# The merge of the next block's inverses emitted ahead of a block's chain, in one layer of a hybrid attention and RWKV-7 encoder

## The chip, the core and the metric

The kernel runs on one core of one Trainium2 chip. Its time is the device time of one execution in microseconds (us); several executions give a median. A core has a matmul engine (TensorE, PE in the profile; its weight loads are shown apart as PEld), a vector engine (DVE), a scalar engine (ACT), GpSimd (POOL), and SyncE (SP), which issues DMA transfers. Each engine works through a queue of its own in order and waits on semaphores for the others.

## The reference

One layer of an encoder over 1024 positions of width 1024: a half-step SwiGLU feed-forward, then a mixing step in which one input projection feeds eight heads of dilated attention and eight heads of RWKV-7, then a second half-step feed-forward. The change lies in the RWKV-7 scan, which runs forward and backward over the sequence:

```python
def _rwkv7_step(state, inp):
    r, w, k, v, kk, kka = inp
    sa = jnp.einsum('dbhvk,dbhk->dbhv', state, kk)
    state = state * w[..., None, :] - sa[..., :, None] * kka[..., None, :] + v[..., :, None] * k[..., None, :]
    y = jnp.einsum('dbhvk,dbhk->dbhv', state, r)
    return state, y
...
    xs = (orient(both(r)), orient(decay), orient(k_dir), orient(both(v)),
          orient(both(kk)), orient(kk[:, :, None, :] * a))
    _, ys = lax.scan(_rwkv7_step, state0, xs)
...
    x = x + post2(concat(attn, rwkv) @ w_out)
```

The two directions' outputs are summed, normalised for each head, given a bonus term and multiplied by a gate (the finishing units below). Both groups then go through `w_out`.

## The kernel before

**The scan in chunks.** The step by step scan is worked in chunks of 64 positions, two chunks to a block, so eight blocks (`NB`), numbered in the order of the scan; both directions of a block are worked together. Inside a chunk the rule is a triangular system for each of the 16 pairs of head and direction. A block passes through four steps.

- *prep* (to L852): DVE and ACT scale the keys by the decays; PE multiplies them (`lp`, L836) and transposes them (`bp`, L844); DVE masks the products into `lm` (L838). The triangles go out to memory and come back as `X`.
- *solve* (L872 to L876): DVE inverts the 32 x 32 diagonal halves of all triangles in 31 steps of two operations, one after the other (`ttmp`, `Ti`); a last transpose (L876) leaves the inverses in `X` again. One solve is a long serial piece of DVE work.
- *merge* (L889 to L902): joins two 32 x 32 inverses to a 64 x 64 one for each of 32 triangles. On PE, 64 transposes (L889) write `pa`; ACT copies it to `tt` (L890); 32 products with the off-diagonal part `lm` go back to `pa` (L894); ACT copies those to `tt` (L896, two copies) and to `am` (L897); 32 products (L900) need both; ACT writes them negated into `tt` (L902, two copies). So PE and ACT alternate. There is one bank for `pa`, one `am`, and two `tt`, used in turn.
- *chain* (L923 to L972): the scan proper. At its start ACT copies part of `pr` into `lm` (L928, four copies; this part must wait until L894 has read its own). Then, for each of the two chunks: `xu` = state times `lm` (L941); ACT copies it to `xs` (L944); the state is started with `st` from `sv` (a helper at L937); `xu` again from `xs` and the merged inverse `tt` (L952); ACT writes `uv` (L954); more `y` and `st` from `uv` (L937); DVE scales `st` to the next state `sv` (L968); ACT copies `y` to `yb` (L970). A chain needs the chain before it through `sv`, and its own merge through `tt`.

The merge is written as follows, shortened:

```python
        tt = self.tt[n % 2]
        T.matmul(pa[r, j, :], D[r, j, :], self.ident[r, r], ...)            # L889, 64 of them
        A.copy(tt[:, :, 32:64], pa)                                         # L890
        T.matmul(pa[hi, j, :], lm[lo, par, d, i, pr, 32:64], D[lo, j, :])   # L894, 32
        A.copy(tt[lo, :, 0:32], pa[lo])                                     # L896, two halves
        A.copy(am, pa)                                                      # L897
        T.matmul(pa[lo, j, :], am[hi, j, :], tt[hi, j, 32:64])              # L900, 32
        A.activation(tt[lo, :, 32:64], pa[lo], AF.Copy, scale=-1.0)         # L902, two halves
```

**What else runs there.** `upto(n + 3)` emits prep and solve up to block n + 3 behind chain n. `project_attended` multiplies finished attention tiles by the upper half of `w_out` (`po`, L1064, large matmuls; inputs `yq`, `yah`, `yal` at L1075 to L1078; the result is copied to `yao` at L1083); its weights are loaded as `wor` and split into two parts `woh` and `wol` (L1054). Such tiles give PE work that needs no chain. Behind the loop come the finishing units: `yc` (L995), `var` (L1004), `bonus` (L1011), `rstd` (L1014), `gate` (L1025) on PE, with DVE and ACT steps between them (L996 to L1026, then a split at L186 and L187), and the lower half of `w_out`, whose weights come as `wor` and are split at L186 and L187 into `woh` and `wol`, for the products `pw` (L1064).

**What sets the order.** The program is written once, and a scheduler with a cost model places each instruction on its engine's queue: among what its model holds ready, the instruction that was emitted first goes first. So the place of a call in the loop is a rank and not a fixed position.

Of the kernel before, what the change touches and what calls it, by code (L numbers as in the profile page):

```python
# [163 lines left out]
class _Kernel:  # L164
# [1002 lines left out]
    def run(self):  # L1167
# [5 lines left out]
        with self.top as top:  # L1173
# [86 lines left out]
            NB, s_sr, s_pr, s_zr, s_pm = NC_ // BLK, ExitStack(), ExitStack(), ExitStack(), ExitStack()  # L1260
# [5 lines left out]
            pm = self.pool(s_pm, "ps_m", 1, space=PSUM, **R)  # L1266
# [4 lines left out]
            blk = {}  # L1271
# [7 lines left out]
            sc = self.pool(s_sc, "scan")  # L1279
# [9 lines left out]
            def upto(m):  # L1289
                while nxt[0] <= min(m, NB - 1):  # L1290
                    n = nxt[0]
                    blk[n] = self.prep(n, sp, pp, (R0, R1, B0)[n % 3])
                    blk[n]["inv"] = self.solve(n, sp)
                    nxt[0] += 1
# [3 lines left out]
            upto(2)  # L1298
            WA = self.out_weights(eo, 0, self.aog)
            for n in range(NB):  # L1300
                if n:
                    self.merge(n, blk[n], sc, pm)
                self.chain(n, blk.pop(n), sc, pc)
                upto(n + 3)
                for t in {0: [0, 1], 1: [2], 2: [3], 3: [4], 4: [5, 6], 5: [7]}.get(n, []):
                    self.project_attended(eo, sc, pe, t, WA, rs_a)
# [133 lines left out]
```

## Time and profile before

| | us |
|---|---|
| runs, median of 3 | 2345.42 (2341.84 to 2350.20) |
| the profiled execution | 2343.05 |
| its span, first to last instruction | 2341.3 |
| granted clock, mean | 0.969 |

The scan stage with its eight chains takes from about 1256 to 1563 us of the span, an eighth of the whole. The two feed-forward parts hold most of the rest, and the change emits nothing there. A row of the timeline gives the start, the length, the engine, the line, the operation, what is written and read, the shape, the number of records, and in brackets how long the engine stood idle before and what released it. A window row gives the busy time of each engine in a stretch, then the clock that PE was granted as a share of full speed, the busy share of the DMA engines, and what they moved.

### The profile page before, as it was taken

How to read it: one execution, taken by the hardware profiler on the slowest of the kernel's cores; microseconds unless marked ns; L12 is line 12 of the kernel's file. 1: busy time of each engine (PE TensorE's matmuls, PEld its weight loads, DVE VectorE, ACT ScalarE, POOL GpSimd, SP SyncE). 2: the span in 40 equal slices, each digit the busy share in tenths (PEclk: the TensorE clock that was granted, in tenths of full speed). 3: DMA queues.
4: the chain of work that ended last, by engine and by line, in shares of the span. 5: the costliest groups of instructions: out<-in, count | busy, mean ns of one | idle time of the engine just before them, and what ended most of it. 6: DMA issues, size and time to landing. Idle time of an engine off the chain costs nothing. (4 is left out here: it accounts for less than half of the span.)

```text
span 2341.3 us, 41376 instructions
## 1 busy us (share of the span) xinstructions
PE 2206.1 (94%) x15556; PEld 1783.6 (76%) x15556; DVE 1768.5 (76%) x2870; ACT 1031.8 (44%) x1958; POOL 551.5 (24%) x662
## 2 busy tenths in 40 slices
PE   6999999999999998999996998988799999999997
PEld 4788888878877676788775777765578888887886
DVE  8899999965676244666668877737899999996565
ACT  4323232354577412666555555454442323235443
POOL 6244444410000010111111111122424444441000
PEclk8999999999999999999997999989899999999999
DMA  5244545486672514443268655467435454548665
GB/s 154 97 165 167 171 148 172 153 269 191 195 229 83 219 46 123 119 115 99 62 174 222 174 155 161 113 205 267 154 113 170 168 171 147 173 154 269 193 191 178
DMA packets 357148, 381.97 MB, mean 163 GB/s; under 512 B 73042, under 2 KB 264402, under 8 KB 356948
## 3 DMA queue, kind: packets, MB, share of 16 engines
q1 hardware_dynamic: 309088, 278.53, 39.5%
q0 software_dynamic: 27504, 88.14, 9.9%
q10 hardware_dynamic: 20356, 12.66, 1.8%
q8 instruction: 122, 2.00, 0.4%
q14 instruction: 78, 0.64, 0.1%
HBM read 256.49 MB, written 122.75 MB: 162 GB/s over the span
## 5 line engine op out<-in xcount | busy, mean ns | idle before, releaser
L186 ACT ACTIVATE wh<-raw 128x512 fp32r<-128x512 f32 (+1 forms) x273 | 168.2, 627 | 271.2 <-DVE raw L62 93.6
L187 DVE TENSOR_TENSOR wl<-raw,wh 128x512 fp32r<-128x512 f32 (+1 forms) x273 | 278.7, 1023 | 6.0 <-ACT wh L186 5.2
L81 PE MATMUL gu<-xh,wh 128*128 128x512 f32 x704 | 278.3, 396 | 1.2 <-ACT xh L186 0.8
L81 PE MATMUL gu<-xl,wh 128*128 128x512 f32 x704 | 276.6, 393 | 0.0
L81 PE MATMUL gu<-xh,wl 128*128 128x512 f32 x704 | 276.2, 392 | 0.0
L415 PE MATMUL pd<-gl,gwh 128*128 128x512 f32 x616 | 240.3, 390 | 2.3 <-DVE gl L187 2.3
L415 PE MATMUL pd<-gh,gwh 128*128 128x512 f32 x616 | 239.5, 390 | 0.6 <-DVE row L86 0.6
L415 PE MATMUL pd<-gh,gwl 128*128 128x512 f32 x616 | 239.7, 389 | 0.0
L86 DVE TENSOR_TENSOR row<-gu,row 128x512 f32<-128x512 f32 x308 | 206.3, 681 | 23.9 <-PE gu L81 23.1
L187 DVE TENSOR_TENSOR gwl<-graw,gwh 128x512 fp32r<-128x512 f32 (+1 forms) x176 | 117.9, 672 | 127.7 <-ACT gwh L186 126.9
L116 POOL DMA_DIRECT2D d_hid<-row x154 | 84.7, 551 | 473.1 <-DVE row L114 447.6
L186 ACT ACTIVATE gwh<-graw 128x512 fp32r<-128x512 f32 (+1 forms) x176 | 101.4, 576 | 186.3 <-PE pd L415 154.3
L81 PEld LDWEIGHTS gu<-xh,wh 128*128 128x128 f32 x704 | 133.9, 190 | 30.1 <-ACT xh L186 2.0
L81 PEld LDWEIGHTS gu<-xl,wh 128*128 128x128 f32 x704 | 133.9, 190 | 27.7
L81 PEld LDWEIGHTS gu<-xh,wl 128*128 128x128 f32 x704 | 133.5, 190 | 27.9
L415 PEld LDWEIGHTS pd<-gl,gwh 128*128 128x128 f32 x616 | 115.6, 188 | 27.4 <-DVE gl L187 3.7
L415 PEld LDWEIGHTS pd<-gh,gwh 128*128 128x128 f32 x616 | 115.5, 188 | 25.3 <-DVE row L86 1.0
L415 PEld LDWEIGHTS pd<-gh,gwl 128*128 128x128 f32 x616 | 115.7, 188 | 24.0
L187 DVE TENSOR_TENSOR gl<-raw,gh 128x512 fp32r<-128x512 f32 x160 | 113.6, 722 | 18.1 <-ACT gh L186 17.7
L94 ACT ACTIVATE row<-row 128x512 f32<-128x512 f32 x44 | 27.9, 633 | 221.6 <-DVE row L86 214.1
L145 POOL TENSOR_TENSOR ws<-ws 128x512 f32<-128x512 f32 x88 | 114.3, 1299 | 1.2
L186 ACT ACTIVATE gh<-raw 128x512 fp32r<-128x512 f32 x160 | 98.0, 621 | 35.3 <-DMA raw<-in_ffn_w_down_dram 25.5
(354 smaller groups left out, 5254.3 us busy)
## 6 DMA issues: line engine op xcount, KB each, us to landing
d_hid<-row POOLq DMA_DIRECT2D x154, 256.0 KB, 2.4
graw<-d_hid SPq DMA_DIRECT2D x132, 256.0 KB, 3.2
raw<-in_ffn_w_gate_dram SPq DMA_DIRECT2D x88, 256.0 KB, 3.1
raw<-in_ffn_w_up_dram SPq DMA_DIRECT2D x88, 256.0 KB, 3.4
ws<-in_ffn_w_down_dram SPq DMA_DIRECT2D x88, 256.0 KB, 4.6
d_ws<-ws POOLq DMA_DIRECT2D x88, 256.0 KB, 2.3
raw<-d_ws SPq DMA_DIRECT2D x88, 256.0 KB, 2.9
raw<-in_ffn_w_down_dram SPq DMA_DIRECT2D x66, 256.0 KB, 3.5
```

The source lines that it names most:

```text
L81: self.K.nc.tensor.matmul(ps, a[:, k, :], b[:, k, :], start=(k == 0 and i == 0), stop=(k == 3 and i == 2))
L86: add = lambda o, x: V.tensor_tensor(o, ps, x, op=OP.add)
L94: A.activation(y[:, 0], y[:, 0], AF.Silu)
L116: put = lambda n, y: G.dma_start(self.hid[n - 1, j // 2], y)
L145: G.tensor_tensor(o, a, b, op=OP.subtract)
L186: self.nc.scalar.activation(h, src, AF.Copy)
L187: (eng or self.nc.vector).tensor_tensor(l, src, h, op=OP.subtract)
L415: T.matmul(ps[x], a[:, ts], b, start=(m == 0 and k == 0), stop=(m == NM - 1 and k == 2))
```

## The change

In the loop over blocks, block n's own merge is no longer emitted ahead of its chain. Block n + 1's is emitted there, so that of the two it is the merge that ranks first. Merge 0 stands ahead of the loop in both. No instruction is added or left out.

```diff
             for n in range(NB):
-                if n:
-                    self.merge(n, blk[n], sc, pm)
+                if n + 1 < NB:
+                    self.merge(n + 1, blk[n + 1], sc, pm)
                 self.chain(n, blk.pop(n), sc, pc)
                 upto(n + 3)
```

Three places in the queues. First PE's queue at the end of the scan. Before, these rows lead from the end of chain 6 (`sv_15958` is the state that it leaves) to chain 7 (`xu_16206`), with merge 7 (`pa_16059`) between them:

```order
L937 MATMUL y_15963<-lm_14420,uv_15955 64x64 x16
L889 MATMUL pa_16059<-ident_62,X_15164 32x32 x4
L937 MATMUL st_16207<-sv_15958,ident_62 64x256 x4
L937 MATMUL y_16208<-pr_15033,sv_15958 64x64 x8
L937 MATMUL y_16208<-pr_15101,sv_15958 64x64 x8
L894 MATMUL pa_16059<-X_15164,lm_15022 32x32 x32
L941 MATMUL xu_16206<-sv_15958,lm_15022 64x64
L900 MATMUL pa_16059<-tt1_11964,am_16058 32x32 x32
L941 MATMUL xu_16206<-sv_15958,lm_15022 64x64 x15
L995 MATMUL yc_16432<-f_y0_16418,k_cen_6989 128x512
L952 MATMUL xu_16206<-xs_16225,tt1_11964 64x64 x16
```

In the changed kernel merge 7 (now `pa_15849`) lies in the first chunk of chain 6 (`y_15998`, `st_15997`), and the second piece shows the end of chain 6 with chain 7 (`xu_16206`) right behind it:

```order
L889 MATMUL pa_15849<-ident_62,X_15300 32x32 x64
L952 MATMUL xu_15996<-xs_16015,tt0_11963 64x64 x2
L937 MATMUL y_15998<-pr_14635,sv_15704 64x64 x5
L894 MATMUL pa_15849<-X_15300,lm_15158 32x32 x32
L937 MATMUL st_15997<-uv_15990,bt_14581 64x64
L937 MATMUL y_15998<-lm_14556,uv_15990 64x64
L937 MATMUL st_15997<-uv_15990,bt_14581 64x64 x7
L937 MATMUL st_15997<-uv_15990,bt_14649 64x64 x8
L937 MATMUL y_15998<-lm_14556,uv_15990 64x64 x8
L900 MATMUL pa_15849<-tt1_11964,am_15848 32x32 x32
```

```order
L937 MATMUL st_16098<-uv_16091,bt_14649 64x64 x8
L937 MATMUL y_16099<-lm_14556,uv_16091 64x64 x15
L941 MATMUL xu_16206<-sv_16094,lm_15158 64x64 x16
L937 MATMUL st_16207<-sv_16094,ident_62 64x256 x4
L937 MATMUL y_16208<-pr_15169,sv_16094 64x64 x5
L952 MATMUL xu_16206<-xs_16225,tt1_11964 64x64 x16
```

The merge's last two steps moved ahead by a whole chain, the same holds for merges 1 to 6, and `yc` of the first finishing unit is no longer in chain 7's first chunk: one `yc` stands in its second, and the rest of that unit behind it.

Second, ACT's queue around merge 2. Before, the copies of merge 2 (`pa_13473`, into `tt0`) stood between prep's and ahead of chain 2's own (`xs_13639`, `uv_13614`):

```order
L890 COPY tt0_11963<-pa_13473 128x16x32
L1084 DMA d_hp_83<-yao_13469 128x512
L928 COPY lm_12117<-pr_12128 64x8x64 x2
L812 ACTIVATE th_w_13820<-th_w_13820 128x512
L846 COPY bt_13309<-bp_13334 128x2x256
L846 COPY bt_13309<-bp_13335 128x2x256
L896 COPY tt0_11963<-pa_13473 32x16x32 x2
L897 COPY am_13472<-pa_13473 128x512
```

Now merge 2 (`pa_13007`) stands among chain 1's copies (`yb_13142` of its first chunk, `xs_13274` and `uv_13249` of its second):

```order
L890 COPY tt0_11963<-pa_13007 128x16x32
L928 COPY lm_12117<-pr_12128 64x8x64
L896 COPY tt0_11963<-pa_13007 32x16x32 x2
L897 COPY am_13006<-pa_13007 128x512
L970 COPY yb_13142<-y_13156 128x4x64
L970 COPY yb_13143<-y_13156 128x4x64
L944 COPY xs_13274<-xu_13255 128x512
L928 COPY lm_12117<-pr_12128 64x8x64
L928 COPY lm_12117<-pr_12196 64x8x64
L902 ACTIVATE tt0_11963<-pa_13007 32x16x32 x2
L928 COPY lm_12117<-pr_12196 64x8x64
L954 ACTIVATE uv_13249<-xu_13255 64x2x256 x2
```

The merge's copies moved into the running chain, between and ahead of that chain's own copies; with merge 1 it is the last `woh` split (L1054) that stands between L890 and L896.

Third, DVE's queue at the first finishing unit (`f_y0_16418`). Before, its last step (L1026) and its split (`xl0`) were followed by the second unit's reciprocal (L1007), and the first weight split (`wol_16646`) came nine rows later:

```order
L1021 TENSOR_TENSOR f_y0_16418<-f_y0_16418,f_v_16428 128x512
L999 SCALAR_TENSOR_TENSOR f_k0_16520<-f_k0_16520,rkc_468,f_r_16524 128x256 x2
L1026 TENSOR_TENSOR f_y0_16418<-f_y0_16418,gate_16461 128x512
L187 TENSOR_TENSOR xl0_16407<-f_y0_16418,xh0_16406 128x2x256
L1007 RECIPROCAL f_rs_16493<-f_rs_16493 128x8
```

Now:

```order
L1021 TENSOR_TENSOR f_y0_16418<-f_y0_16418,f_v_16428 128x512
L187 TENSOR_TENSOR wol_16646<-wor_16643,woh_16645 128x512
L1026 TENSOR_TENSOR f_y0_16418<-f_y0_16418,gate_16461 128x512
L187 TENSOR_TENSOR wol_16652<-wor_16649,woh_16651 128x512
L187 TENSOR_TENSOR xl0_16407<-f_y0_16418,xh0_16406 128x2x256
L1007 RECIPROCAL f_rs_16493<-f_rs_16493 128x8
```

Two weight splits moved in front of the unit's last steps; on ACT their first halves (`woh`, L186) moved likewise.

## The prediction, made before the run

> **What bounds the kernel now.** I read the first part of the page, then the busy time by stage, then the waits of PE inside the scan stage, then the timeline around single merges. The first part of the page:
>
> ```profile
> span 2341.3 us, 41376 instructions
> ...
> PE 2206.1 (94%) x15556; PEld 1783.6 (76%) x15556; DVE 1768.5 (76%) x2870; ACT 1031.8 (44%) x1958; POOL 551.5 (24%) x662
> ```
>
> PE sets the pace of the whole. The change touches only the scan stage, so the windows by stage come next (columns: window, its length, then busy time of PE, PEld, DVE, ACT, POOL with instruction counts, granted clock, DMA share, GB/s): blocks 2 to 5, then chains 6 and 7, then the finishing units.
>
> ```profile
> 1349.00:1511.00 162.00, 146.50 (x2900) 122.55 (x2897) 125.97 (x367) 83.67 (x160) 22.46 (x41) 0.94 0.52 145
> 1511.00:1563.00 52.00, 46.98 (x1172) 38.72 (x1172) 18.08 (x46) 27.03 (x51) 14.82 (x17) 0.93 0.62 189
> 1563.00:1631.00 68.00, 58.38 (x228) 38.19 (x226) 49.14 (x77) 35.37 (x72) 15.79 (x13) 0.90 0.79 267
> ```
>
> In the four steady blocks PE is busy 146.5 of 162 us, DVE only 126, so PE's own queue is what a block costs (162 / 4 = 40.5 us), and the change can win idle PE time and lost clock, nothing else: the number of matmuls is the same. How much of that hangs on the merge is in the groups of 1349 to 1511 (busy us, mean ns, then idle of PE just before them and its releaser; every small matmul leaves two records):
>
> ```profile
> L889 PE MATMUL pa<-ident,X 32*32 32x32 f32 x520 | 8.9, 208 | 3.3 <-issue 1.8 <-ACT tt L902 1.4
> L900 PE MATMUL pa<-tt,am 32*32 32x32 f32 x256 | 5.3, 192 | 0.2 <-ACT am L897 0.2
> L894 PE MATMUL pa<-X,lm 32*32 32x32 f32 x256 | 5.2, 192 | 0.9 <-ACT tt L890 0.9
> L890 ACT COPY tt<-pa 128x512 f32<-128x512 f32 x4 | 2.4, 590 | 0.0
> ```
>
> The merges cost only 4.4 us of waiting there. One of the waits, 1.42 us, and two more are seen in the timeline (start, length, instruction, idle before):
>
> ```profile
> 1334.69 0.85 PE L889 MATMUL pa<-ident,X 32*32 32x32 f32 x44 [1.85 <-issue]
> ...
> 1372.73 0.64 PE L889 MATMUL pa<-ident,X 32*32 32x32 f32 x30 [1.42 <-ACT tt L902]
> ...
> 1456.11 1.04 DVE L876 STREAM_TRANSPOSE X<-Ti 128x512 f32<-128x512 f32 x1
> ...
> 1457.26 0.33 PE L889 MATMUL pa<-ident,X 32*32 32x32 f32 x16 [1.83 <-issue]
> 1457.52 1.85 PE L937 MATMUL st<-uv,bt 128*64 128x64 f32 x29
> ...
> 1508.94 1.09 PE L937 MATMUL st<-uv,bt 128*64 128x64 f32 x29
> 1509.92 1.10 PE L937 MATMUL y<-lm,uv 128*64 128x64 f32 x29
> ```
>
> The "issue" wait at 1457.26 is really for DVE: the solve's last instruction, the transpose that makes X, ends at 1456.11 + 1.04 = 1457.15. And behind these waits the same 29 records take 1.85 instead of 1.09 us. The granted clock (the number after POOL's) says why:
>
> ```profile
> 1374.00:1382.00 8.00, 8.00 (x170) 7.08 (x167) 4.28 (x8) 2.37 (x6) 0.00 (x0) 0.50 0.65 186
> 1457.00:1461.00 4.00, 3.74 (x76) 3.73 (x76) 3.36 (x7) 0.00 (x0) 1.72 (x3) 0.57 0.22 66
> 1541.00:1549.00 8.00, 4.92 (x97) 3.92 (x96) 0.81 (x2) 4.91 (x9) 2.52 (x2) 0.62 1.06 329
> ```
>
> So a wait of 1.4 to 1.9 us costs itself and then 4 x (1 - 0.57) = 1.7 us, in the worst case 8 x (1 - 0.50) = 4.0 us, of slow clock.
>
> [...]
>
> **The steady blocks, part by part.** Nothing is added or removed; merge n+1 now stands inside chain n instead of behind it. In the order of PE all of it (64 L889, 32 L894, 32 L900) lies there; before, only L889 did, wholly or in part.
>
> Removed: the wait on L902, 1.4 us, since the two merges' copies no longer follow each other so closely; the 0.9 us on L890 and 0.2 us on L897; and the 4.0 us of slow clock behind the first of these. Sum 6.5 us.
>
> Not removed: the two waits for X (1.85 and 1.83 us) and their 1.7 us of clock each, 7.1 us together. The order of DVE's solve hardly changes, and PE comes to L889 no later than before.
>
> Added: inside a chain the merge's three steps pass through ACT. L889 to L894 needs the L890 copy, 0.59 us; L894 to L900 needs three ACT copies. Their length and the gap they leave are in the one merge of the trace that has no cover, merge 7, with the rows of PE around it (ACT's rows first):
>
> ```profile
> 1540.57 1.16 ACT L896 COPY tt<-pa 32x512 f32<-32x512 f32 x2
> 1541.74 0.58 ACT L897 COPY am<-pa 128x512 f32<-128x512 f32 x1
> ...
> 1535.59 1.15 PE L937 MATMUL y<-lm,uv 128*64 128x64 f32 x31
> ...
> 1537.38 1.08 PE L937 MATMUL st<-sv,ident 64*64 64x256 f32 x8 [0.45 <-DVE sv L968]
> ...
> 1539.32 1.20 PE L894 MATMUL pa<-X,lm 32*32 32x32 f32 x64
> 1540.71 0.33 PE L941 MATMUL xu<-sv,lm 128*64 128x64 f32 x2 [0.20 <-ACT lm L928]
> 1542.38 1.43 PE L900 MATMUL pa<-tt,am 32*32 32x32 f32 x57 [1.33 <-ACT am L897]
> 1545.55 0.42 PE L900 MATMUL pa<-tt,am 32*32 32x32 f32 x7 [1.74 <-issue]
> 1545.90 1.97 PE L941 MATMUL xu<-sv,lm 128*64 128x64 f32 x30
> ```
>
> From L894's end (1540.52) to L900 at 1542.38 are 1.86 us. In the new order 21 to 27 of the chain's small matmuls stand between the two in merges 2 to 6. At 1.09 us for 29 records, 0.075 us a matmul, they cover 1.6 to 2.0 us. So little is uncovered if ACT is free when L894 ends: 0 to 0.3 us; if ACT has one more copy in front (0.6 us), 0.6 to 0.9. I take 0.4 us for each of five merges, 2.0 us. The bounds are 0 and, with no cover, the tail's 0.20 + 1.33 = 1.5 us. A wait of 0.4 us is far below the 1.42 that slowed the clock, so I add no clock.
>
> Merge 1 is a case of its own: on ACT, L896 now stands behind the last attention weight's split (L1054), which waits for a load.
>
> ```profile
> 1300.45 0.34 SPq L182 DMA_DIRECT2D wor<-in_w_out_dram  x1
> ...
> 1304.26 0.72 ACT L1054 ACTIVATE woh<-wor,c_attn_out_g 128x512 fp32r<-128x512 f32 x1
> ```
>
> Solve 1 and with it L889 are ready at about 1300, so L894 can end near 1303.3. L1054 ends at 1304.98, and 1.74 us of copies put L900 at 1306.7; six st and sixteen y matmuls cover 22 x 0.075 = 1.7 us. 3.4 - 1.7 = 1.7; four lp matmuls stand in between too, so I take 1.5 us (0 if the load is early).
>
> Blocks: -6.5 + 2.0 + 1.5 = **-3.0 us** (bounds -13.6, with no added wait and none for X, and, with no cover in the six merges of the blocks, 6 x 3.2 - 6.5 = +12.7, priced with the second rival).
>
> **The tail.** Before, chain 6's last matmul ends at 1535.59 + 1.15 = 1536.74, and chain 7's xu matmuls start at 1545.90: merge 7 lies bare between, with 0.45 + 0.20 + 1.33 + 1.74 = 3.7 us of idle PE, the window at clock 0.62 behind them. Now merge 7 lies in chain 6. Its L894 and L900 (1.2 us each by L894's row) lengthen that chain to 1539.1. Chain 7 follows after the 0.45 us on sv, at 1539.6. A chunk without foreign work is read from chain 5:
>
> ```profile
> 1504.55 1.15 PE L941 MATMUL xu<-sv,lm 128*64 128x64 f32 x30
> ...
> 1562.57 1.13 PE L1025 MATMUL gate<-f_sg,g2w 128*128 128x256 f32 x4
> 1563.53 1.02 PE L995 MATMUL yc<-f_y,k_cen 128*128 128x512 f32 x2
> 1565.62 1.05 PE L1004 MATMUL var<-k_ones,f_y 128*128 128x2 f32 x8 [1.07 <-ACT f_y L996]
> ...
> 1569.01 1.62 PE L1025 MATMUL gate<-f_sg,g2w 128*128 128x256 f32 x4
> ...
> 1567.01 0.20 DVE L1007 RECIPROCAL f_rs<-f_rs 128x8 f32<-128x8 f32 x1 [1.20 <-ACT f_rs L1006]
> ...
> 1578.07 0.69 DVE L187 TENSOR_TENSOR wol<-wor,woh 128x512 fp32r<-128x512 f32 x1
> ...
> 1578.79 5.93 DMA wor<-in_w_out_dram
> ...
> 1591.81 3.68 DMA wor<-in_w_out_dram
> ```
>
> It runs from 1504.55 to 1511.02 (the end of the y row at 1509.92), 6.5 us. Two of them and the one yc pair (1.0 us) that stays among them end chain 7 at 1539.6 + 14.0 = 1553.6, where it ended at about 1562.6. That 9 us isn't the gain, because the first finishing unit hid in chain 7 and now mostly follows it. From var's start to gate's end a unit takes 1565.62 to 1570.63, 5.0 us; so unit 1's yc comes at 1558.5 instead of 1563.53: 5.0 us won.
>
> Part of this goes back. In DVE's new order two splits of the output weight (wol) stand around unit 0's last step, and SP issues their load only when unit 0's bonus matmuls have freed their operands, two steps of PE after 1553.6, about 1555.6. With 3.68 to 5.93 us on the way (the two last rows) it lands at 1560.4 in the mean; ACT's half of the split 0.6, wol 0.7, the last step 0.7, the second wol 0.7 and xl 0.7 put unit 1's reciprocal at 1563.8 instead of 1567.01. So 3.2 us are left: **-3.2 us** (bounds -5.0, the load hidden; and 0, a later landing or a slow clock while PE waits).
>
> **Sum.** -3.0 - 3.2 = -6.2 us. The profiled execution took 2343.05 us (span 2341.3), so 2336.85; it lay 2.37 us under the median of the runs shown, 2345.42, so the runs' time is **2339.2 us**. A change below 0.3%, 7.0 us, can't be told from none here: faster is below 2338.4, slower above 2352.5. My value lies at that border.
>
> **The rivals.**
>
> *All of it works.* The waits for X vanish too, since chain work stands in front of them (7.1 us more), ACT's copies are covered, and the load is hidden: -13.6 - 5.0 = -18.6, that is 2326.8. For it: DVE is only 78% busy in the blocks (126 / 162), so X could come earlier. Against: X's time is set by DVE, not by where the merge stands.
>
> *Slower: the merge stalls the chain.* PE takes its queue in order, so where L900 waits for ACT, the chain's st, y and the next chunk behind it wait too. If cover fails at all seven merges, since the chain's own xs and uv copies (L944, L954) share ACT's queue with the merge's, each costs 1.5 us and drops the clock for 1.7 us: 7 x 3.2 = 22.4, less 6.5 and 3.2, +12.7, that is 2358.1. It decides when a merge costs over (6.5 + 3.2) / 7 = 1.4 us. For it: waits of this size did slow the clock at 1372.73 and 1457.26. Against: 1.6 to 2.0 us of cover against 1.86.
>
> [...]
>
> *It does not do what it says.* Most of L889 stood in the previous chain already; the blocks stay paced by X, and the weight load takes the tail's gain back: 0 us, 2345.4.
>
> **How the numbers follow.** Forecast 0.45, its own range 2332 to 2346, split about evenly at 2338.4 (0.21 faster, 0.24 same). All of it works 0.17, faster. Stalled chain 0.30, slower. Not doing what it says 0.08 (0.06 same, 0.02 slower). Faster 0.38, same 0.30, slower 0.32. The range takes in most of both outer cases, 2321 to 2360; beyond it I leave about a quarter of the first (0.04) and 0.4 of the second (0.12).
>
> **What would show it.** Right: PE's idle before L900 in the blocks below 0.6 us a merge; the two waits on X at L889 still there; chain 7's xu within a microsecond of chain 6's end; chain 7 done 7 to 9 us earlier relative to chain 6, but unit 1's reciprocal only some 3 us. Wrong: idle of 1.3 us or more before L900 in each block with the granted clock at 0.5 to 0.6 behind it, a block of over 41 us, or the finishing units standing on the weight load for more than 4 us.

## The result, and the profile after

| | median of 12 runs, us | lowest to highest |
|---|---|---|
| before | 2344.49 | 2333.62 to 2353.00 |
| changed | 2345.22 | 2337.53 to 2349.34 |

The ratio of changed to before is 0.9998, with a 95% interval of 0.9984 to 1.0012: no change that can be measured, to within some 3 us either way. The profiled execution of the changed kernel has a span of 2343.4 us, and its page starts with nearly the same shares as before:

```profile
span 2343.4 us, 41364 instructions
...
PE 2204.7 (94%) x15556; PEld 1783.2 (76%) x15556; DVE 1766.4 (75%) x2870; ACT 1032.5 (44%) x1958; POOL 552.9 (24%) x662
```

The windows by stage (columns as above) are cut at about the ends of chains 0, 5, 6 and 7, and some 50 us behind. The first four rows are of before, the next four of the changed kernel:

```profile
1304.00:1511.00 207.00, 188.04 (x3684) 156.58 (x3684) 165.43 (x486) 107.52 (x205) 28.09 (x52) 0.94 0.54 150
1511.00:1537.00 26.00, 24.70 (x690) 20.48 (x689) 11.12 (x34) 12.00 (x23) 4.75 (x8) 1.00 0.30 86
1537.00:1563.00 26.00, 22.28 (x482) 18.24 (x483) 6.95 (x13) 15.04 (x29) 10.07 (x9) 0.87 0.93 291
1563.00:1611.00 48.00, 41.68 (x161) 24.82 (x160) 36.21 (x58) 27.61 (x57) 14.30 (x11) 0.89 0.81 262
```

```profile
1312.00:1519.00 207.00, 187.49 (x3696) 156.10 (x3692) 162.89 (x481) 110.08 (x209) 27.70 (x52) 0.94 0.53 145
1519.00:1546.00 27.00, 24.10 (x620) 19.93 (x618) 10.33 (x29) 12.50 (x25) 4.77 (x9) 1.00 0.28 81
1546.00:1565.00 19.00, 16.60 (x344) 13.69 (x344) 3.14 (x6) 6.17 (x13) 6.93 (x7) 0.91 1.03 315
1565.00:1616.00 51.00, 41.28 (x158) 25.98 (x158) 35.40 (x61) 28.03 (x54) 17.54 (x14) 0.88 0.83 259
```

Chains 1 to 5 took 207 us in both, with the same busy PE. Chain 7, the third row, fell from 26 to 19 us. So the time did move, only its sum didn't. The sums that follow are cut at fixed events of one execution: the end of solve 0 (DVE's transpose), the ends of the chains' last output copies (yb, L970), and the end of the last matmul with the lower half of w_out (pw). Each kernel of the two was profiled twice, the second time with the experiments (e10, e11). "Code waits" are explained below.

| us | solve 0 to chain 5 | chain 6 | chain 7 | chain 7 to last pw | sum | code waits |
|---|---|---|---|---|---|---|
| before | 255.4 | 25.7 | 25.9 | 101.8 | 408.8 | 1.7 |
| before, again | 255.6 | 25.7 | 26.1 | 99.5 | 406.9 | 2.2 |
| changed | 260.8 | 26.9 | 18.8 | 103.7 | 410.2 | 11.8 |
| changed, again | 258.6 | 27.1 | 18.1 | 103.5 | 407.3 | 14.4 |

What comes after the last pw takes 674.6 to 676.1 us in all four. The means: the blocks lost 259.7 - 255.5 = 4.2 us; from chain 5 to the last pw 152.4 became 149.1, 3.3 us won. The sum is +0.9 us, well inside the interval.

Two remarks on the blocks. Their loss lies ahead of chain 1's end (93.5 and 92.9 us from solve 0 before, 99.7 and 100.4 changed). From there to chain 5's end, with all but the same PE records (2886 and 2884), the changed kernel took 161.1 and 158.2 us against 161.9 and 162.7, so chains 2 to 5 won 2.7 us in the mean. And the changed kernel has one merge more ahead of chain 5's end (4544 PE records against 4344), but that isn't the loss: PE's busy time there, without what half clock added, is 201.3 and 202.2 us against 202.2 and 200.8. What grew is PE's idle time, from 30.7 and 26.6 to 33.4 and 35.4 us. Three experiments below keep the order of one of the two kernels up to chain 5 and agree with its sums: 257.7 us in e1 (as before), 262.1 in e4 and 261.7 in e7 (as changed).

**Where the blocks' waits went.** The waits of PE up to chain 5's end that bear on this (engine, line, what it waited for: us in total, times, longest), first before, then changed:

```profile
PE lp L836 <- DVE lm L838: 7.8, 9, 2.2
...
PE pa L889 <- issue: 3.7, 2, 1.8
PE pa L894 <- ACT tt L890: 3.7, 2, 2.7
PE xu L952 <- ACT xs L944: 2.6, 2, 1.6
PE pa L900 <- ACT am L897: 2.2, 2, 1.9
PE st L937 <- ACT uv L954: 2.2, 2, 1.2
...
PE pa L889 <- ACT tt L902: 1.4, 1, 1.4
```

```profile
PE pa L894 <- issue: 7.5, 3, 3.3
PE lp L836 <- DVE lm L838: 4.7, 5, 1.8
...
PE pa L894 <- ACT tt L890: 2.7, 1, 2.7
PE pa L889 <- issue: 2.4, 1, 2.4
PE pa L900 <- ACT am L897: 1.9, 1, 1.9
...
PE xu L952 <- ACT xs L944: 1.1, 2, 0.7
...
PE pa L889 <- DVE X L876: 0.9, 2, 0.5
PE st L937 <- ACT uv L954: 0.7, 1, 0.7
```

The wait on L902 is gone, the one wait that is left on L890 (2.7 us) and on L897 (1.9 us) is merge 0's, and the waits on lm, xs and uv fell by 3.1, 1.5 and 1.5 us. (In the second pair of executions the first two fell alike, from 6.8 to 3.8 and from 2.9 to 1.1, that on uv only from 2.9 to 2.5.) In their place stands one that was not there: L894 waiting 7.5 us with no releaser. It falls in the middle of a run of one line, as in merges 2 and 4 (timeline of PE):

```profile
1342.82 0.79 PE L894 MATMUL pa<-X,lm 32*32 32x32 f32 x38
1346.87 0.56 PE L894 MATMUL pa<-X,lm 32*32 32x32 f32 x22 [3.25 <-issue]
...
1425.78 0.57 PE L894 MATMUL pa<-X,lm 32*32 32x32 f32 x24
1428.32 0.82 PE L894 MATMUL pa<-X,lm 32*32 32x32 f32 x40 [1.98 <-issue]
```

All 64 records of such a run need the same copy and the same inverses, so no tile is late. What comes in during the pause is shown by the DMA queues of 1343.6 to 1346.9 (queue, kind: packets, MB, share), and for the whole execution by the page:

```profile
q8 instruction: 1, 0.02, 2.1%
...
q8 instruction: 122, 2.00, 0.4%
```

Queue 8 carries code: 122 transfers of 16 KB, against 15556 + 15556 PE records, so one transfer holds 255 of them, 128 matmul records with their weight loads. The single packets of that queue stand in the trace with their times; beside them PE's pauses of over 0.25 us inside a run:

```
pause of PE (changed kernel)      transfer of 16 KB on queue 8     its end to PE's next record
1305.0 to 1307.3, 2.30 us, L894   1304.29 to 1305.71               1.55 us
1343.6 to 1346.9, 3.25 us, L894   1344.46 to 1345.54               1.32 us
1426.3 to 1428.3, 1.98 us, L894   1426.05 to 1426.98               1.34 us
1466.4 to 1468.8, 2.39 us, L889   1466.24 to 1467.47               1.35 us
1532.4 to 1533.4, 0.96 us, L894   1530.92 to 1531.80               1.55 us
```

PE stood still until its own code had come, and went on 1.32 to 1.55 us after the end of a transfer. That the queue carries PE's code is shown by its count in other runs: 125 transfers in e4 below, which adds 768 PE records, and 114 in e5 and e6, which take 2048 away, 256 to a transfer each time. "Code waits" in the tables are the pauses that end 1.1 to 1.6 us after such a transfer. Five of the seven pauses are listed; the other two are of 0.45 and 0.48 us. For the one of 0.48 us and for the 1.0 us of e13 below, both at L836, the profile names DVE as releaser, so these two may not be code. Before, large po matmuls stood between most of a merge's pieces (twelve of them, from 1325.82 to 1328.84 us, between an L894 and an L900), which, as I read it, gave the next transfer time: code waits sum to 1.7 us there, against 11.8. In the changed kernel a merge inside a chain makes one long run of small ones.

**The tail.** PE's timeline at the end of chain 7 in the changed kernel, then a row each of SP, POOL and ACT:

```profile
1553.27 0.33 PE L941 MATMUL xu<-sv,lm 128*64 128x64 f32 x2 [0.41 <-issue]
1555.20 1.54 PE L995 MATMUL yc<-f_y,k_cen 128*128 128x512 f32 x2 [1.60 <-POOL f_y L994]
...
1564.19 1.05 PE L1004 MATMUL var<-k_ones,f_y 128*128 128x2 f32 x8
...
1568.86 0.66 PE L1014 MATMUL rstd<-ident,f_y 128*128 128x128 f32 x4 [2.65 <-ACT f_y L1008]
...
1545.94 1.02 SPq L182 DMA_DIRECT2D f_y<-d_y  x2
...
1553.89 1.26 POOL L994 TENSOR_TENSOR f_y<-f_y,f_y 128x512 f32<-128x512 f32 x1 [6.70 <-issue]
...
1566.15 1.28 ACT L1006 ACT_TABLE_LOAD   x1 [1.21 <-issue]
```

Chain 7's second chunk stands behind yc, and yc waits for POOL's sum of two loads that SP starts only when chain 6's last matmul has freed their buffers (SP stood 48.0 us for it): 1555.20 is 9.7 us after chain 6's end. Before, these loads start behind chain 6 as well, but merge 7 and chain 7's first matmuls fill the time, and yc comes 11.1 us after chain 6's end without a wait. Then unit 0's var, rstd and gate come behind the chain, uncovered, with a table load of ACT on their way (1.28 us, the last row) that chain 7 had hidden before (1.28 us at 1552.21).

### The profile page after: what moved, and what is told of

It is laid out like the page before. It is cut to its first block, busy times and chain, and to the rows that moved or that the text cites. A ratio compares the mean times of both kernels' runs of the same rounds, so it can differ in the third digit from the quotient of the medians.

```text
span 2343.4 us, 41364 instructions
## 1 busy us (share of the span) xinstructions
PE 2204.7 (94%) x15556; PEld 1783.2 (76%) x15556; DVE 1766.4 (75%) x2870; ACT 1032.5 (44%) x1958; POOL 552.9 (24%) x662
## 5 line engine op out<-in xcount | busy, mean ns | idle before, releaser
L186 ACT ACTIVATE wh<-raw 128x512 fp32r<-128x512 f32 (+1 forms) x273 | 167.5, 626 | 261.2 <-DVE raw L62 92.2
L186 ACT ACTIVATE gwh<-graw 128x512 fp32r<-128x512 f32 (+1 forms) x176 | 101.3, 576 | 186.7 <-PE pd L415 152.2
L186 ACT ACTIVATE gh<-raw 128x512 fp32r<-128x512 f32 x160 | 98.1, 621 | 36.4 <-DMA raw<-in_ffn_w_down_dram 21.7
```

Source lines behind the costliest of these rows:

```text
L186: self.nc.scalar.activation(h, src, AF.Copy)
```

## The experiments

The theory after this reading: the early merges trade waits on ACT and DVE for waits on code; the tail wins, and part of it is given back to yc's loads and to the uncovered first unit. All sums are from one profiled execution, ratios from the runs.

**Merge 7 alone early** (e1_last).

```diff
-                if n + 1 < NB:
-                    self.merge(n + 1, blk[n + 1], sc, pm)
+                if 0 < n < 7:
+                    self.merge(n, blk[n], sc, pm)
+                if n == 6:
+                    self.merge(7, blk[7], sc, pm)
```

> Merge 7 alone is emitted ahead of chain 6, merges 1 to 6 stand as before. Theory (PE's instruction fetch): in the changed kernel PE waits 2 to 3 us in the middle of runs of L894 with no releaser in the profile, each time until about 1.3 us after a 16 KB transfer of its instruction queue; dense small matmuls use up their code faster than it comes. That costs merge 1's place in chain 0 (+5.4 us) and eats the gain of merges 2 to 6, while merge 7's place wins 7.1 us between the ends of chains 6 and 7, of which the finishing units give back about 2. So this kernel should end chain 7 about 6 us earlier than before, counted from the end of solve 0, and take about 2340 us beside a before of 2344.5 (-0.2%). Rival (the finishing units are held by their weight loads whatever chain 7 does): chain 7 ends earlier but the last pw matmul does not, no change, 2344.5. Rival (noise: blocks and tail both unchanged): chain 6 to 7 still about 26 us.

Measured: 257.7 us to chain 5, then 32.3, 22.9 and 100.0; ratio to before 1.0009 (0.9992 to 1.0026). No gain. Merges 6 and 7 now both lie in chain 6, and its timeline has a code wait, a wait on ACT behind it, records that take longer than usual, and in chain 7 yc:

```profile
1531.15 0.63 PE L894 MATMUL pa<-X,lm 32*32 32x32 f32 x28
1533.33 0.76 PE L894 MATMUL pa<-X,lm 32*32 32x32 f32 x36 [1.54 <-issue]
1534.01 0.56 PE L952 MATMUL xu<-xs,tt 64*64 64x64 f32 x12
1535.95 1.92 PE L900 MATMUL pa<-tt,am 32*32 32x32 f32 x64 [1.38 <-ACT am L897]
...
1557.79 2.07 PE L995 MATMUL yc<-f_y,k_cen 128*128 128x512 f32 x2 [4.77 <-POOL f_y L994]
```

The second rival in the prediction, a merge that stalls its chain, is seen here in one place: L900 stood 1.38 us for the copy L897 and then took 1.92 us where 1.20 is usual. Chain 7 ended 55.2 us after chain 5, later than before (51.6 and 51.8), so none of the three expectations describes this run, and the one that the tail's gain stands by itself fell.

**All but merge 1 early** (e2_late1): in the changed loop, merge 1 is emitted ahead of chain 1 again.

```diff
-                if n + 1 < NB:
+                if n == 1:
+                    self.merge(1, blk[1], sc, pm)
+                if 0 < n < 7:
                     self.merge(n + 1, blk[n + 1], sc, pm)
```

> As the changed kernel, but merge 1 stands ahead of its own chain again, so that chain 0 runs without it. Theory: chain 0's 5.4 us are caused by merge 1 inside it and are gone, the rest stays: 5 us below the changed kernel, about 2340 us. Rival (the work of merge 1 is only shifted and reappears ahead of chain 1): as the changed kernel, 2345.

Measured: chain 0 ended 46.5 us after solve 0 (53.7 and 48.8 in the changed kernel), but chain 1, which now held merges 1 and 2, took 54.0 us instead of 46.0 and 51.5. To chain 5 it is 262.5 us; ratio 1.0011 (0.9997 to 1.0026). The rival holds: the cost of merge 1 is only shifted. This run also speaks against reading the blocks' loss off the code waits alone: 5.7 us of them are left up to chain 5, about half of the changed kernel's, and the blocks are no shorter.

**Merge 1 alone early** (e3_first).

```diff
-                if n + 1 < NB:
-                    self.merge(n + 1, blk[n + 1], sc, pm)
+                if n == 0:
+                    self.merge(1, blk[1], sc, pm)
+                if n > 1:
+                    self.merge(n, blk[n], sc, pm)
```

> Merge 1 alone is emitted ahead of chain 0, the other merges as before. Theory: chain 0 ends 5.4 us later than before counted from solve 0's end, and nothing gains it back: about 2350 us (+0.2%). Rival (shifted only): chain 1's end is back at its place, 2344.5.

Measured: chain 0 at 51.5 us, 2.6 to 3.3 later than before, but chain 1 at 88.3, some 5 earlier (93.5 and 92.9), and chain 5 at 258.6. Ratio 1.0006 (0.9994 to 1.0019). Again the rival in the main: the cost is shifted, and what chain 1 had won was lost again by chain 5.

**A long run of small matmuls** (e4_rep): merge 7 of the changed kernel issues its transposes four times.

```diff
-        for j in range(NI):
+        for j in [j for _ in range(4 if n == 7 else 1) for j in range(NI)]:
```

> As the changed kernel, but merge 7 issues each of its L889 transposes four times (the same values are written again), 512 records instead of 128, all of them ready once X is there. In the changed kernel 128 such records took 1.29 us, 10 ns each. Theory (fetch): 16 KB of code are 128 matmul records with their weight loads, and the transfers follow each other in 3.6 to 3.8 us at best, so the run of 512 should take 12 to 15 us, in pieces of at most 128 records with waits between them that show no releaser. Rival (no such limit; the mid-run waits come from another engine's semaphore): one piece, about 5.2 us.

The timeline of PE at that merge:

```profile
1532.16 1.59 PE L889 MATMUL pa<-ident,X 32*32 32x32 f32 x164
1535.83 1.28 PE L889 MATMUL pa<-ident,X 32*32 32x32 f32 x128 [2.08 <-issue]
1539.57 1.93 PE L889 MATMUL pa<-ident,X 32*32 32x32 f32 x128 [2.47 <-issue]
1543.59 1.49 PE L889 MATMUL pa<-ident,X 32*32 32x32 f32 x92 [2.09 <-issue]
```

From 1532.16 to 1545.08 are 12.9 us for 512 records: 164, then pieces of exactly 128, 3.7 to 4.0 us apart, then the rest. A piece itself takes 1.28 us (the second row; 1.29 us for 128 in the changed kernel, at 1340.77 and granted clock 1.00). The execution took 2359.24 us. My estimate of the limit from these rows is 3.7 us / 128, about 29 ns a record: in such a run, records that need less outrun their code. The merge's records are below it, at 10 ns (L889, 128 in 1.28 us) and 19 ns (L894, 64 in 1.20 us); the chain's own are above, at 36 to 38 ns (xu, 32 in 1.15 us; st, 29 in 1.09 us).

**The transposes off PE** (e5_afterT in the changed order, e6_beforeT in the old one, each profiled again as e12 and e13). One DVE transpose in 32 x 32 blocks writes what 64 small matmuls and a copy made.

```diff
-        for j in range(NI):
-            for r in [r for lo, hi in lohi for r in (hi, lo)]:
-                T.matmul(pa[r, j, :], D[r, j, :], self.ident[r, r], start=True, stop=True)
-        A.copy(tt[:, :, 32:64], pa)
+        self.nc.vector.transpose(tt[:, :, 32:64], D)
+        for lo, hi in lohi:
+            A.copy(tt[lo, :, 0:32], tt[lo, :, 32:64])
...
         for lo, hi in lohi:
-            A.copy(tt[lo, :, 0:32], pa[lo])
-        A.copy(am, pa)
+            A.copy(am[hi], pa[hi])
```

> The changed kernel with the merge's 64 small transposes taken off PE: one DVE transpose of 128 x 512 in 32 x 32 blocks (1.06 us each in the solve) writes the same values straight into tt, so that L889 and the copy L890 are gone, 128 records of PE and one 16 KB piece of its code for each merge. Theory (fetch): most of the 11.8 us of mid-run waits go, since a piece is then used up no faster than the next one comes, besides the 1.3 us of matmul time in each of eight merges (10 us): 2345 - 10 - 8 = about 2327 us, and mid-run waits that end 1.3 to 1.5 us after a transfer of code sum to under 4 us. Rival (the mid-run waits have another cause, such as the merge's place in the queue): they stay at about 10 us, and only PE's 10 us are won, less what DVE adds: 2335 to 2340.

> The same edit in the kernel of before, which had only 1.7 us of such waits. Theory (fetch): only PE's matmul time is won, at most 10 us: 2335 to 2340, so 8 us or so slower than the same edit in the changed kernel; the changed order is then the better of the two. Rival: both gain the same and stay equal within 0.15%.

> The changed order with the transposes on DVE once more, for the spread of single executions. Theory (code waits are what the changed order lost in the blocks, and its tail is what it lost against the old order): from solve 0's end to chain 5's end 244 to 249 us (259.7 in the mean of the changed kernel's two executions), from there to the last pw matmul 148 to 152. Rival (the order of the two is chance): 249 to 253 and 140 to 146.

> The old order with the transposes on DVE once more. Theory: from solve 0's end to chain 5's end 249 to 252 us (255.5 in the mean of the two executions of before), from there to the last pw matmul 139 to 143. Rival (chance): 244 to 249 and 148 to 152.

| us | solve 0 to chain 5 | chain 6 | chain 7 | chain 7 to last pw | sum | code waits | ratio to before |
|---|---|---|---|---|---|---|---|
| e5, changed order | 246.4 | 27.1 | 23.2 | 100.0 | 396.7 | 0 | 0.9942 (0.9924 to 0.9961) |
| e12, the same | 249.5 | 27.1 | 23.2 | 100.5 | 400.5 | 0 | |
| e6, old order | 250.4 | 23.7 | 23.5 | 93.4 | 391.1 | 0 | 0.9908 (0.9888 to 0.9927) |
| e13, the same | 247.1 | 23.3 | 23.5 | 93.2 | 387.1 | 1.0 | |

DVE's new transposes cost 0.7 us each (the group of its line in e6):

```profile
L887 DVE STREAM_TRANSPOSE tt<-X 128x512 f32<-128x512 f32 x8 | 5.7, 710 | 0.1
```

In the blocks the code waits are gone, the changed order won 11.7 us there (259.7 to 248.0 in the means) and the old one 6.7 (255.5 to 248.8), so the changed order's deficit of 4.2 us went away together with its code waits. That they alone had made it isn't shown: 5 us more for some 12 us of code waits removed says that most of the rest was taken up by other waits, the same edit takes 64 matmuls and a copy out of each merge, and the repeats' 249.5 and 247.1 us lie where the rival, chance, had put them. In the tail the repeats are as the theory said, and the forecast of e6 that the changed order would come out ahead fell: it is the slower by 10 us there (150.6 against 140.3 from chain 5 to the last pw). As whole times, e5's ratio makes it 2331 us, between its theory (2327) and its rival (2335 to 2340); e6 is below both of its values.

Chain 7 takes the same 23 us in both, because yc's loads set its length. In e6:

```profile
1537.08 2.07 PE L993 MATMUL yc<-f_y,k_cen 128*128 128x512 f32 x2 [5.00 <-POOL f_y L992]
```

That is 9.8 us after chain 6's end again (10.0 in e5). Merge 7 lies inside chain 6 in both: with its transposes off PE, the cost model put it there in e6 too, although the loop emits it behind chain 6. Its last step stands in three pieces in e6 and in one in e5 (lines are two lower here than above):

```profile
1519.90 0.74 PE L898 MATMUL pa<-tt,am 32*32 32x32 f32 x18
...
1524.95 0.25 PE L898 MATMUL pa<-tt,am 32*32 32x32 f32 x4
...
1527.20 0.88 PE L898 MATMUL pa<-tt,am 32*32 32x32 f32 x42
```

```profile
1517.86 1.20 PE L898 MATMUL pa<-tt,am 32*32 32x32 f32 x64 [1.82 <-ACT am L895]
```

Only the last 42 records of it, 0.9 us, lie behind chain 6's last matmul in e6. So the 3.6 us by which chain 6 is longer in e5 (27.1 against 23.5) aren't the price of an early merge 7 as such. Part of it is the wait of 1.82 us for a copy, and 11 more of the large po matmuls lie in e5's chain 6 (24 against 13). Of the 7 us behind chain 7, 3.4 to 5.1 are slow clock (by the clock records of the trace, against none in e6 and e13); why the clock held there wasn't tried and stays open. The kernel e6_beforeT is the fastest of all here, 0.9% below before.

**yc held behind chain 7** (e7_pin on the changed kernel; e8_best on e6 with merge 7 alone early).

```diff
+        if n == 7:
+            self.cen7 = c.tile([128, 2, 4, 64], F32, name="xs", tag="xs").rearrange("p a b t -> p (a b t)")[:, 0:128]
+            V.scalar_tensor_tensor(self.cen7, YB[1][:, 0, :], 0.0, self.cen, op0=OP.mult, op1=OP.add)
...
-        T.matmul(yc, self.cen, y, start=True, stop=True)
+        first = b == self.blocks[0] and g == 0
+        T.matmul(yc, self.cen7 if first else self.cen, y, start=True, stop=True)
```

> The changed kernel, with the first finishing unit's yc matmul made to need chain 7's last output (its matrix is rewritten by DVE as itself plus 0 times that output), so that it can't stand inside chain 7. In all four runs with merge 7 inside chain 6, yc waited 1.6 to 4.9 us there for its loads, which start only when chain 6 frees their buffers (9.7 us from the end of chain 6 to yc in the changed kernel), and the chain stood behind it. Theory (this wait is where the tail's gain stops): chain 7 ends 14 to 16 us after chain 6 instead of 18.8, and the last pw matmul comes 2 to 4 us earlier, 2342 us beside the change's 2345 (about 0.1%, at the edge of what can be told). Rival (the unit is only put off and the finishing units take as much longer): chain 7 is as much earlier, the last pw matmul stays, 2345 us.

> The kernel of before with the merge's transposes on DVE, merge 7 alone ahead of chain 6, and yc held behind chain 7. Theory: with no code waits and no wait of yc the move of merge 7 now pays, some 5 us below the same kernel with all merges late: ratio to before about 0.989, 2317 us. Rival (the order at the tail makes no difference): ratio 0.991 as there, 2321 us.

Measured: chain 7 took 14.8 us in e7 and 15.5 in e8, as forecast, but chain 6 took 30.2 and 26.1 us, some 3 more than without the hold (27.0 and 23.5), and the stage behind chain 7 111.6 and 111.3 us, 8 to 18 more. Ratios to before: 1.0026 (1.0010 to 1.0042) and 0.9949 (0.9929 to 0.9969). The rival of e7 holds and more, and e8 lies above both of its values. It is also less of a test of merge 7's place than it was meant to be, since merge 7 lay in chain 6 in e6 already; what moved is its last step, now in one piece. Putting unit 0 off costs more than the chain gains, which points to unit 0's start, and not chain 7's end, as what the rest of the stage hangs on; but half clock cost 11.9 us behind chain 7 in both runs, against 8.5 in the changed kernel and none in e6, so a part of the loss is clock. A yc that blocks the chain is the cheaper of the two.

**The two kernels once more** (e10, e11), for the spread; the sums are in the first table.

> The changed kernel once more, for the spread of single executions. If the sums are properties of the kernel, chain 7 again ends 18 to 20 us after chain 6, yc waits 1 to 5 us, and the mid-run waits on code sum to 8 to 15 us; if they are chance, chain 6 to 7 may be anywhere from 18 to 26.

> The kernel of before once more. Property of the kernel: chain 7 ends 25 to 27 us after chain 6, no wait of yc, mid-run waits on code below 4 us. Chance: anything from 18 to 26 us.

Chain 7's 18.8 and 18.1 against 25.9 and 26.1 us, and code waits of 12 to 14 against 2, are properties of the kernels. Single sums over the blocks vary by 2 to 3 us.

## Why the prediction's range held although both of its terms missed

The forecast was 2339.2 us, 0.27% below the median it started from. Measured is 0.02% less, with an interval from 0.16% less to 0.12% more, so the forecast itself lies outside the interval; its own range, 2332 to 2346 us, held 2345.2 close to the upper end. The rival that nothing comes of it had named 2345.4 us, which is nearer, but its mechanism (blocks paced by X, units standing on the weight load) isn't what the runs show either. Of the signs that were named, the short waits before L900, chain 7's xu 0.6 us behind chain 6 and chain 7's gain of 7 to 8 us came; the two waits for X and the earlier reciprocal of unit 1 didn't. By steps:

- *Removed waits.* Right in kind: the wait on L902 went, and those on L890 and L897 inside the blocks. Waits on lm and xs, which were not on my list, fell too, it seems because PE came to them later.
- *The two waits for X stay.* Not borne out: 3.7 us became 0.9, and one of the two places became a code wait of 2.39 us. But in the second pair they were 0.9 before and 1.0 after, so part of this is the spread of single executions.
- *Added: 0.4 us a merge on L900.* The cover held better than that: between the ends of chains 0 and 5 no wait on L897 is left. ACT's copies in the chain's queue cost nothing there that the waits show, so the slower rival's mechanism didn't come about in the changed kernel's blocks.
- *Merge 1: 1.5 us for the weight load ahead of L896.* Wrong place. L1054 didn't wait for its load; L894 stopped for code, 2.30 us. Chain 0 took 53.7 and 48.8 us instead of 48.9 and 48.2, and up to chain 1's end the changed kernel lost 7 us in the mean.
- *Blocks -3.0.* This step failed: they measured +4.2. The steady part, chains 2 to 5, won 2.7 us where 4.5 (6.5 - 2.0) were forecast, and it won them by less half clock, not by shorter waits: PE's idle time there was 15.5 and 13.0 us before and 15.7 and 16.2 after. The part up to chain 1's end lost 7 instead of 1.5. The term that was missing is code: 10 to 12 us more of it in the whole scan, after merges that I had packed into chains without asking how fast PE can be fed. The pauses and their cause are shown; that they make up the whole loss isn't, since e2 with half of them is no faster there. The sign was in the profile of before, unread: its wait of 1.74 us inside L900 at 1545.55, put down as idle time of a bare merge, ends 1.42 us after a code transfer, as the experiments' do.
- *Tail -3.2.* From chain 5's end to the last pw -3.3 was measured, and that agreement is luck. The forecast ended at unit 1's reciprocal, which was to come 6.2 us earlier by both terms together. Counted from solve 0's end it came after 318.1 and 315.7 us, where before it came after 310.7 and 311.1, so some 6 us later. From there to the last pw the changed kernel then took 5 us less (92 against 97 in the means), which no step of the prediction contains and whose cause wasn't tried. Chain 6 grew by 1.3 us, not 2.4: I had counted merge 7 in, but not that merge 6's last steps leave chain 6 at the same time. Chain 7 took 18.1 to 18.8 us, not 14.5, since yc waited for loads that I had taken as landed. ACT stood only 1.1 us for the weight load; what stood ahead of unit 1 is the uncovered first unit.
- *The clock.* A slow stretch of 1.7 us behind each wait was the right size in two of the changed kernel's five from the end of chain 0 to chain 5; the other three cost 3.4, 3.4 and 5.1 us. The sum hardly moved: from solve 0 to the last pw 39.2 and 39.7 us were lost to half clock before, 41.1 and 35.9 after.

So both terms missed up to unit 1's reciprocal, by some 12 us together, and about 5 us came back behind it. That the time still fell into the range is owed to the range's width and to that part, not to the mechanism.

## What to carry to other kernels

Count a stretch's instructions as well as its microseconds: here the merge's records took 10 and 19 ns while e4's came in pieces of 128 every 3.7 to 4.0 us, packing them together turned other waits into waits on code (2 us of them became 12 to 14), and taking instructions away (one DVE transpose for 64 small matmuls, 0.9% in e6) won what reordering didn't. A wait with no releaser in the middle of a run of one line (3.25 us at 1343.6) was the sign. When a bare stretch is closed, look for what starts at its end: here yc came 9.6 to 10.4 us after chain 6's end in all nine executions in which it waited for its loads inside chain 7, whatever else chain 7 did. And before a part of a kernel is compared by itself, see where the scheduler has put it: an order in the source is a rank, and in e6 merge 7 moved without being told to.

## What the runs showed of the hardware that was not expected

- PE's code came in 16 KB transfers while the program ran, 122 in the execution, 128 matmul records with their weight loads to a transfer. In the dense run of e4 PE's pieces of 128 records follow each other in 3.7 to 4.0 us, with four transfers in the 12 us from 1533 to 1545. In the changed kernel's execution the closest two transfers start 3.5 us apart, each takes 0.9 to 2.0 us on the queue (median 1.05), and PE went on 1.32 to 1.55 us after the end of one in the five pauses listed above.
- The granted clock is 1.0 or 0.5 in every clock record of the profiled executions of before and of the changed kernel, and the half-clock stretches of the scan are multiples of 3.4 us. In the changed kernel, from chain 0's last microseconds to chain 5, half clock: 6.8 us from 1306.6, 3.4 from 1347.6, 3.4 from 1429.5, 6.8 from 1439.7 and 10.2 from 1470.4. No pause of PE ahead of these stretches was longer than 3.25 us. In the 3.4 us ahead of each of the five, PE was busy for 21 to 52% of the time. What sets the start and the length of such a stretch was not shown.
